# Float32r value products and batched modulation columns in the even layer of a two-layer hybrid attention kernel

## The chip, the cores and the metric

The kernel runs on one core of a Trainium2 chip. The metric is device time in microseconds. TensorE (PE, with its weight loads shown as PEld), VectorE (DVE), ScalarE (ACT), GpSimd (POOL) and the DMA queues (issued here mostly by SyncE, SP) each work through their own instructions in order and wait for one another by semaphores.

## The reference, cut to what matters

The program is one inference step of two layers over 128 prompt and 512 sample tokens with 1024 features. The part at stake is the attention of the even layer, 16 heads of 64 values: 8 latent heads (MLA, each with its own values) and 8 grouped heads (GQA, four heads share a value head). Sample queries read 128 cached and 512 own keys; prompt queries read only the 128 prompt keys.

```
def block(qi):
    s = jnp.einsum('bqhgd,bthd->bhgqt', qi, k).astype(jnp.float32) * scale
    p = jax.nn.softmax(s, axis=-1).astype(v.dtype)
    return jnp.einsum('bhgqt,bthd->bqhgd', p, v)
...
o_a = attend(q_a, k_a, v_a).reshape(B, S, MLA_W) * jax.nn.silu(g_a)
o_b = attend(q_bg, kb_all, vb_all).reshape(B, S, GQA_W) * jax.nn.silu(g_b)
return jnp.concatenate([o_a, o_b], axis=-1) @ w_out, new
```

The odd layer's input is a normalised x times a gain plus a shift; both come from the condition vectors by a product with 2048 columns of a modulation weight ("modulation columns").

## The kernel before, in words

All results are kept to float32 accuracy. Where a product runs in float32r, an operand is split into an upper part (rounded to float32r) and a lower part (the rest), and the products of the parts are added up in PSUM.

`even_attention` goes through 16 heads (h = 0 to 15; MLA first). A head has four sample query tiles of 128 queries and five key tiles of 128 keys. For each query tile, `head_scores` makes scores `s` [128 queries, 640 keys] (float32r products, L596) in one of two PSUM tiles; `softexp` takes the row maximum on VectorE (L603) and the exponential with its row sum on ScalarE (L606), the reciprocal of the sum on VectorE (L609); GpSimd multiplies the probabilities `p` by it (L616). For each key tile k, `head_T` transposes four blocks of `p` on TensorE (L623) into a PSUM tile `t1` (two of them), and one engine copies that into `pT` [128 keys, 512 queries] (ScalarE, L628; VectorE for k = 2, L626). `head_PV` multiplies with the 64 value columns (L634): two float32 products of 256 queries each, one into partitions 0 to 63 of PSUM tile `o`, one into 64 to 127, so that they lie side by side in the array. In the trace each float32 product is two PE instructions, so a key tile has four. At a head's end, VectorE multiplies the two halves of `o` into the gates `og` (L710).

`attention` writes the order out by hand: the transposition of key tile k+1 stands ahead of the value product of key tile k, and scores run about one head ahead (`more_scores`); a scheduler that simulates the program then fixes each engine's final order. Prompt heads are done four at a time by `prompt_quad` in four stages, spread over the first heads (two stages ahead of head 0, then two in each head), so that all four quads lie in the MLA half. `prep` (queries and keys of head h+2: a copy L760, transpositions, a split L315 or L754) and `side(h)` ride along. For h < 8, `side` calls `ada_cols` for the odd layer's modulation columns: 8 products and two transpositions on TensorE, then on VectorE a reduction (L186) and three operations on [128, 2] columns (L190, L193, L195). For h >= 8 it makes partial rows of the even gate (`ada_gate_part`), splits half of `og` for the output projection (`op_split`, ScalarE and VectorE L842) and, in heads 12 to 15, loads the four weight tiles of the projection's first 512 columns (`op_load` through `wload`: DMA, upper part on ScalarE L76, lower part on GpSimd L77).

Behind the attention, `mid` runs the output projection: `out_proj` first multiplies the first half of `og` (heads 0 to 7) of all five token tiles with weight tiles 0 and 1 (60 products, L83 to L85), then the second half with tiles 2 and 3.

Of the kernel before, what the change touches and what calls it, by code (L numbers as in the profile page):

```python
# [10 lines left out]
F32 = mybir.dt.float32  # L11
F32R = mybir.dt.float32r
# [25 lines left out]
class K:  # L38
# [3 lines left out]
    # ---------------------------------------------------------------- helpers  # L42
# [8 lines left out]
    def sumsq(self, src, n, w):  # L51
        """sum of squares over groups of w: src [128, n*w] in SBUF -> [128, n]"""
# [14 lines left out]
    def wload(self, src, n, w, pool=None, pre="w", bufs=2, cp=None):  # L67
        """stream a [128, n, w] weight tile and split it into two float32r parts"""
# [18 lines left out]
    def lin_tok(self, pieces, ncols, hh, hl, toks, evac, pool, tag="acc", bufs=5):  # L87
        """out[token, col] for token tiles toks; pieces: [(dram ap, nk)]"""
# [12 lines left out]
    def drain(self, toks, evac, lag=3):  # L101
        """evacuate psum; what evac returns is done lag tiles later"""
# [9 lines left out]
    def lin_feat(self, src, hh, hl, pool, tag="acc", bufs=5):  # L112
        """out[col (128), token (640)] in two psum tiles of 320 tokens"""
# [9 lines left out]
    def silu_from(self, out, src, shape, pool, other=None):  # L123
        """out = silu(src) (times other); src may be PSUM"""
# [8 lines left out]
    def rope(self, out, x, cos, sin, nh, w, pool, rep=1, dup=False):  # L133
        """out = rope(x), [128, nh, w] views; cos, sin [128, w / rep]"""
# [26 lines left out]
    # ---------------------------------------------------------------- adaLN  # L161
# [8 lines left out]
    def ada_cols(self, L, kk, pool, tag, bufs, raws=None, split=False):  # L170
        """shift and gain of feature tile kk as [128, 2] columns (sample, prompt)"""
# [10 lines left out]
        def rest():  # L182
            for i in range(2):
                nc.tensor.transpose(ps[:, 256 + 128 * i:384 + 128 * i], part[:, i * 128:i * 128 + 128], self.ident)
            red = self.st.tile([128, 2, 2], F32, tag="adar", name="adar", bufs=2)
            nc.vector.tensor_reduce(out=red, in_=ps[:, 256:512].rearrange("p (i g j) -> p i j g", i=2, g=4)[:, :, 0:2],  # L186
                                    axis=AX.X, op=ALU.add)
            vg, vs, vc = (V_EG, V_EBS, V_EBC) if L == "e" else (V_OG, V_OBS, V_OBC)
# [11 lines left out]

    def ada_gate_part(self, L, kk, pool, tag, bufs):
        """partial rows of the gate of feature tile kk"""
# [11 lines left out]
    def ada_gate_row(self, L, pool, tag, bufs):  # L214
        """sum of the partial rows of the gate, to DRAM"""
# [12 lines left out]
    def ada_gate_bc(self, L, to):  # L228
        """gate broadcast over partitions: [128, 2, 1024], sample and prompt"""
        self.gate = to  # L230
        for c in range(2):
            self.nc.sync.dma_start(to[:, c], self.gd[L][c:c + 1].to_broadcast([128, 1024]))

    # ---------------------------------------------------------------- body
    def run(self):
        tc, nc, A = self.tc, self.nc, self.A
        with ExitStack() as es:
# [12 lines left out]
            self.GS = {L: (main.tile([128, 8, 2], F32, name="G" + L), main.tile([128, 8, 2], F32, name="S" + L))  # L250
                       for L in "eo"}
# [27 lines left out]
    # ---------------------------------------------------------------- even layer  # L279
# [1357 lines left out]
```

## Time and profile before

| | us |
|---|---|
| runs: median, lowest, highest of 3 | 910.01, 910.0, 910.73 |
| profiled execution: span from its first to its last instruction | 905.8 |
| median of the runs less that span (what lies around it) | 4.2 |
| busy in the span: PE, DVE, ACT, POOL | 852.9, 541.2, 422.6, 396.6 |
| attention of the even layer, from 229 to 403 us of the span | 174 |

No time of the profiled execution beside its span is given, so the span is set against the runs. An engine's busy time is the time in which one of its instructions is shown as running; a PE instruction's shown length includes the way through the array, so PE is nearly always shown as busy, and what PE costs has to be read from the distance between starts.

### The profile page before, as it was taken

How to read it: one execution, taken by the hardware profiler on the slowest of the kernel's cores; microseconds unless marked ns; L12 is line 12 of the kernel's file. 1: busy time of each engine (PE TensorE's matmuls, PEld its weight loads, DVE VectorE, ACT ScalarE, POOL GpSimd, SP SyncE). 2: the span in 40 equal slices, each digit the busy share in tenths (PEclk: the TensorE clock that was granted, in tenths of full speed). 3: DMA queues.
4: the chain of work that ended last, by engine and by line, in shares of the span. 5: the costliest groups of instructions: out<-in, count | busy, mean ns of one | idle time of the engine just before them, and what ended most of it. 6: DMA issues, size and time to landing. Idle time of an engine off the chain costs nothing.

```text
span 905.8 us, 14374 instructions
## 1 busy us (share of the span) xinstructions
PE 852.9 (94%) x5418; PEld 707.2 (78%) x5418; DVE 541.2 (60%) x1125; ACT 422.6 (47%) x928; POOL 396.6 (44%) x302
## 2 busy tenths in 40 slices
PE   6999899979999999999999999999999899999997
PEld 2778788879776766668887889889989688778786
DVE  3773831993866877641386735077774736666765
ACT  5354523311655677752263324266554656443422
POOL 0144424751754646725535333422221946354930
PEclk9999999999999999999999999999999999999999
DMA  9821222220221222324412212222123122142503
GB/s 347 330 65 35 88 87 71 70 71 24 94 94 53 84 98 93 119 77 176 152 47 105 86 71 94 81 70 71 47 93 129 58 88 63 55 164 75 163 1 117
DMA packets 29641, 88.52 MB, mean 98 GB/s; under 512 B 3752, under 2 KB 6880, under 8 KB 29572
## 3 DMA queue, kind: packets, MB, share of 16 engines
q1 hardware_dynamic: 25904, 83.64, 26.4%
q10 hardware_dynamic: 3668, 3.96, 1.3%
q8 instruction: 43, 0.70, 0.3%
q14 instruction: 26, 0.21, 0.1%
HBM read 80.90 MB, written 6.68 MB: 97 GB/s over the span
## 4 chain that ended last, share of the span: by engine, by line
PE 74%; DVE 16%; issue 3%; ACT 3%; POOL 2%; DMA 1%; SPq 0%; POOLq 0%; ACTq 0%; DVEq 0%
PE acc L84 11%; PE acc L85 11%; PE acc L83 11%; PE s L596 7%; PE acc L1060 6%; PE o L634 5%; PE t L623 5%; PE acc L120 3%; PE o L1146 2%; PE pv L1460 2%; PE ada L177 1%; POOL wlo L77 1%; DVE nm L603 1%; PE gps L210 1%; PE acc L544 1%
## 5 line engine op out<-in xcount | busy, mean ns | idle before, releaser
L77 POOL TENSOR_TENSOR wlo<-raw,whi 128x1024 fp32r<-128x1024 f32 (+4 forms) x79 | 185.8, 2357 | 229.8 <-ACT whi L76 222.7
L85 PE MATMUL acc<-whi,Hl 128*128 128x512 f32 (+2 forms) x400 | 148.5, 373 | 1.6 <-DVE Hl L958 1.6
L84 PE MATMUL acc<-wlo,Hh 128*128 128x512 f32 (+2 forms) x400 | 149.2, 373 | 0.2 <-POOL wlo L77 0.2
L83 PE MATMUL acc<-whi,Hh 128*128 128x512 f32 (+2 forms) x400 | 138.9, 374 | 1.0 <-ACT qk L1064 1.0
L76 ACT CAST whi<-raw 128x1024 fp32r<-128x1024 f32 (+4 forms) x71 | 71.6, 1010 | 131.2 <-PE acc L85 80.5
L603 DVE TENSOR_REDUCE nm<-s 128x1 f32<-128x640 f32 (+1 forms) x104 | 80.9, 780 | 57.1 <-PE s L596 56.0
L616 POOL TENSOR_TENSOR p<-p,rs 128x640 f32<-128x640 f32 x64 | 79.7, 1256 | 64.2 <-DVE rs L609 62.6
L606 ACT ACTIVATE p<-s,nm 128x640 f32<-128x640 f32 (+1 forms) x104 | 79.4, 764 | 59.8 <-DVE nm L603 53.9
L85 PEld LDWEIGHTS acc<-whi,Hl 128*128 128x128 f32 x400 | 75.3, 188 | 14.7 <-DVE Hl L958 1.8
L83 PEld LDWEIGHTS acc<-whi,Hh 128*128 128x128 f32 x400 | 75.1, 188 | 14.0 <-ACT qk L1064 1.2
L84 PEld LDWEIGHTS acc<-wlo,Hh 128*128 128x128 f32 x400 | 75.4, 188 | 12.9 <-POOL wlo L77 0.6
L48 POOL TENSOR_TENSOR rs_r<-rs_h,mhalf 128x1 f32<-128x1 f32 (+4 forms) x39 | 35.6, 921 | 53.4 <-DVE rs_h L47 45.0
L623 PEld LDWEIGHTS t<-cst,p 128*128 128x128 f32 x320 | 34.6, 140 | 23.6 <-issue 22.1
L623 PE MATMUL t<-cst,p 128*128 128x128 f32 x320 | 51.3, 283 | 0.2 <-POOL p L616 0.2
L84 PE MATMUL acc<-wlo,oh 128*128 128x512 f32 (+1 forms) x124 | 48.1, 388 | 0.1
L85 PE MATMUL acc<-whi,ol 128*128 128x512 f32 (+1 forms) x124 | 47.8, 386 | 0.0
L83 PE MATMUL acc<-whi,oh 128*128 128x512 f32 (+1 forms) x124 | 46.7, 389 | 0.0
L628 ACT COPY pT<-t 128x512 f32<-128x512 f32 x64 | 37.1, 584 | 17.4 <-PE t L623 17.0
L120 PE MATMUL acc<-Hh,whi 128*128 128x320 f32 x128 | 31.3, 316 | 6.9 <-DVE og L129 6.9
L63 DVE TENSOR_REDUCE ssq<-sq 128x2 f32<-128x128 f32 (+3 forms) x19 | 11.5, 604 | 40.6 <-ACT sq L61 40.4
L885 ACT ACTIVATE junk<-xt 128x512 bf16<-128x512 f32 (+1 forms) x21 | 12.8, 610 | 49.0 <-DVE xt L883 37.7
L1060 PE MATMUL acc<-Hh,whi 128*128 128x320 f32 x128 | 32.5, 323 | 0.5 <-ACT v L1037 0.5
(380 smaller groups left out, 1983.2 us busy)
## 6 DMA issues: line engine op xcount, KB each, us to landing
adaw<-in_eada_ss_dram SPq DMA_DIRECT2D x16, 512.0 KB, 10.3
raw<-in_oada_ss_dram SPq DMA_DIRECT2D x16, 512.0 KB, 4.3
raw<-in_e_wG_dram SPq DMA_DIRECT2D x8, 512.0 KB, 3.3
raw<-in_eada_g_dram SPq DMA_DIRECT2D x8, 512.0 KB
raw<-in_e_wO_dram SPq DMA_DIRECT2D x8, 512.0 KB, 4.2
raw<-in_oada_g_dram SPq DMA_DIRECT2D x8, 512.0 KB, 3.5
raw<-in_o_wO_dram SPq DMA_DIRECT2D x8, 512.0 KB, 3.9
xT<-in_xT_dram SPq DMA_DIRECT2D x8, 320.0 KB, 5.8
```

The costliest lines, as they stand in the source:

```text
L76: (cp or nc.scalar.copy)(hi[:, 0:m], raw[:, 0:m])
L77: nc.gpsimd.tensor_tensor(out=lo[:, 0:m], in0=raw[:, 0:m], in1=hi[:, 0:m], op=ALU.subtract)
L83: mm(out, lhsT=lh, rhs=rh, start=first, stop=False)
L84: mm(out, lhsT=lh, rhs=rl, start=False, stop=False)
L85: self.mark = mm(out, lhsT=ll, rhs=rh, start=False, stop=last)
L120: mm(acc[j][:, 0:320], lhsT=a[:, k], rhs=b[:, k, j * 320:j * 320 + 320], start=f, stop=l)
L596: self.mark = self.nc.tensor.matmul(out[:, j, 0:w], lhsT=q[0:rows, qcols], rhs=k[0:rows, a:a + w], start=i == 0, stop=i == len(passes) - 1)
L603: nc.vector.tensor_reduce(out=nm, in_=s, axis=AX.XY, op=ALU.max, negate=True)
L606: nc.scalar.activation(out=p[:, 0:n].rearrange("p (a b) -> p a b", a=s.shape[1]), in_=s, func=AF.Exp, bias=nm, accum_out=sm)
L616: self.nc.gpsimd.tensor_tensor(out=p, in0=p, in1=rs.to_broadcast([128, 640]), op=ALU.mult)
L623: self.nc.tensor.transpose(tp[:, i * 128:i * 128 + 128], p[i][:, k * 128:k * 128 + 128], self.ident)
L1060: nc.tensor.matmul(acc[j][:, 0:320], lhsT=a[:, k], rhs=b[:, k, j * 320:j * 320 + 320], start=f, stop=l)
```

## The change

- Value products: each head's value columns are split into upper and lower parts that lie side by side, 128 columns (`values(h)`, one head ahead; for a GQA head only every fourth; the prompt's values `Pa`, `Pb` at the start). `head_T` ends in `split_T`: ScalarE writes the upper part of the transposed probabilities and VectorE the lower part. `head_PV` makes two float32r products of 512 queries, one with each part. Rows 0 to 63 of `o` then hold the upper-value sums and rows 64 to 127 the lower-value sums; at the head's end ScalarE copies the lower half, VectorE adds, GpSimd multiplies into the gates. `prompt_quad` is changed in the same way.
- Normalisation: the reciprocal is taken for two query tiles at once.
- The odd layer's shift and gain: `ada_cols` keeps only the reduction; `ada_close` finishes all eight feature tiles with three operations.
- `op_split` of the first half writes its lower part on GpSimd instead of VectorE.
- The projection's weight tiles 2 and 3 are loaded behind the attention (in `mid`, in a pool `R1b`), not in heads 14 and 15.
- Comments and docstrings are taken out, with no effect on the program.

```diff
         def rest():
...
-            red = self.st.tile([128, 2, 2], F32, tag="adar", name="adar", bufs=2)
+            red = self.gs[L][:, :, kk] if L == "o" else self.st.tile([128, 2, 2], F32, tag="adar", name="adar", bufs=2)
...
+            if L == "o":
+                return
...
+    def ada_close(self):
+
+        G, S = self.GS["o"]
+        col = lambda a: self.cols[:, a:a + 8, None].to_broadcast([128, 8, 2])
+        tt = self.nc.vector.tensor_tensor
+        tt(out=S, in0=S, in1=col(V_OBS), op=ALU.add)
+        tt(out=G, in0=G, in1=col(V_OBC), op=ALU.add)
+        self.nc.vector.scalar_tensor_tensor(out=G, in0=G, scalar=1.0, in1=col(V_OG), op0=ALU.add, op1=ALU.mult)
...
     def head_scores(self, T, ps, passes, i):
...
-        p, rs = self.softexp(T, s, 640, 10)
-        self.nc.gpsimd.tensor_tensor(out=p, in0=p, in1=rs.to_broadcast([128, 640]), op=ALU.mult)
+        if i % 2 == 0:
+            self.pair = [], T.tile([128, 2], F32, tag="sm", name="sm2", bufs=4)
+        tiles, sm = self.pair
+        p = self.softexp(T, s, 640, 10, sm[:, i % 2:i % 2 + 1])
+        tiles.append(p)
+        if i % 2:
+            nc.vector.reciprocal(sm, sm)
+            for j, x in enumerate(tiles):
+                nc.gpsimd.tensor_tensor(out=x, in0=x, in1=sm[:, j:j + 1].to_broadcast([128, 640]), op=ALU.mult)
...
-        pT = T.tile([128, 512], F32, tag="pT", name="pT", bufs=3)
-        if k == 2:
-            self.nc.vector.tensor_copy(pT, tp)
-        else:
-            self.nc.scalar.copy(pT, tp)
-        return pT
...
+        return self.split_T(T, tp)
+
+    def split_T(self, T, tp):
+        parts = [T.tile([128, 512], F32R, tag=n, name=n, bufs=2) for n in ("pTh", "pTl")]
+        self.split_psum(*parts, tp)
+        return parts
...
-            self.nc.tensor.matmul(o[64 * j:64 * j + 64, 0:256], lhsT=V[:, k, col:col + 64],
-                                  rhs=pT[:, 256 * j:256 * j + 256], start=k == 0, stop=k == 4,
-                                  tile_position=(0, 64 * j))
+            self.nc.tensor.matmul(o, lhsT=V(k), rhs=pT[j], start=k == 0 and j == 0, stop=k == 4 and j == 1)
...
                 if k == 2:
                     side(h)
+                    if h + 1 < nh:
+                        self.values(h + 1)
...
-            for j in range(2):
-                g = self.og[r, h // 2, 128 + 256 * j:384 + 256 * j]
-                nc.vector.tensor_tensor(out=g, in0=o[64 * j:64 * j + 64, 0:256], in1=g, op=ALU.mult)
+            s = T.tile([128, 512], F32, tag="os", name="os", bufs=1)
+            nc.scalar.copy(s[r], o[64:128])
+            nc.vector.tensor_tensor(out=s[r], in0=o[0:64], in1=s[r], op=ALU.add)
+            g = self.og[r, h // 2, 128:640]
+            nc.gpsimd.tensor_tensor(out=g, in0=s[r], in1=g, op=ALU.mult)
...
+        def split(out, src):
+            self.nc.vector.tensor_copy(out[..., 0, :], src)
+            self.nc.gpsimd.tensor_tensor(out=out[..., 1, :], in0=src, in1=out[..., 0, :], op=ALU.subtract)
...
+        def values(h):
+
+            if h < 8 or h % 4 == 0:
+                Sa[h] = T.tile([128, 5, 2, 64], F32R, tag="Sa", name="Sa", bufs=2)
+                split(Sa[h], Va[:, 0:5, 64 * h:64 * h + 64] if h < 8 else Vb[:, 0:5, 16 * (h - 8):16 * (h - 8) + 64])
+            else:
+                Sa[h] = Sa[h - 1]
+
+        self.values = values
+        values(0)
+        split(Pa, heads(Va[:, 5]))
+        split(Pb, heads(Vb[:, 5]))
...
-            if h >= 12:
+            if h in (12, 13):
                 self.op_load("e_wO", 0, h - 12)
...
-        self.nc.vector.tensor_tensor(out=lo, in0=src, in1=hi, op=ALU.subtract)
+        (self.nc.vector if m else self.nc.gpsimd).tensor_tensor(out=lo, in0=src, in1=hi, op=ALU.subtract)
...
+        self.Rb = self.tc.alloc_tile_pool(name="R1b", bufs=1, side="right", reuse_waits="tile")
+        for i in (2, 3):
+            self.op_load("e_wO", 0, i)
```

## Rows read from the trace of the kernel before

**Rows 1.** Windows: stretch, length, busy time (count) per engine, granted clock, DMA share, GB/s.

```profile
216.00:229.00 13.00, 11.72 (x77) 10.94 (x76) 6.02 (x14) 4.08 (x10) 1.39 (x2) 1.00 0.00 0
229.00:240.00 11.00, 9.55 (x86) 7.15 (x84) 9.59 (x19) 7.24 (x22) 10.06 (x9) 1.00 0.28 97
229.00:334.00 105.00, 102.26 (x818) 73.07 (x816) 77.23 (x168) 65.92 (x166) 61.90 (x50) 1.00 0.23 82
334.00:403.00 69.00, 67.28 (x542) 42.28 (x541) 43.32 (x85) 47.69 (x101) 40.31 (x29) 1.00 0.32 109
229.00:403.00 174.00, 169.54 (x1358) 115.35 (x1357) 120.55 (x252) 113.61 (x266) 102.22 (x79) 1.00 0.26 93
403.00:417.00 14.00, 14.00 (x64) 11.52 (x63) 3.17 (x6) 3.91 (x6) 1.22 (x1) 1.00 0.48 188
```

**Rows 2.** Chain that ended last, 250 to 285 us: start, length, what.

```profile
253.56 0.87 PE t L623 x8
...
268.42 1.01 PE o L634 x8
...
271.56 0.89 PE s L596 x6
...
280.97 0.58 PE o L634 x4
281.55 0.59 PE t L623 x4
```

**Rows 3.** Timeline of PE, 269 to 272 us: start, length, instruction.

```profile
269.86 0.60 PE L623 MATMUL t<-cst,p 128*128 128x128 f32 x4
270.21 0.83 PE L596 MATMUL s<-Ka,qh 96*128 96x320 f32 x4
270.88 0.46 PE L596 MATMUL s<-Ka,ql 96*128 96x320 f32 x2
271.18 0.38 PE L184 MATMUL ada<-cst,adap 128*128 128x128 f32 x2
```

**Rows 4.** VectorE groups by line and shape, 229 to 403 us: busy, mean ns | idle before.

```profile
L710 DVE TENSOR_TENSOR og<-o,og 64x256 f32<-64x256 f32 x32 | 13.4, 418 | 8.8 <-PE o L634 8.4
L626 DVE COPY pT<-t 128x512 f32<-128x512 f32 x16 | 10.9, 684 | 0.7 <-PE t L623 0.4
L609 DVE RECIPROCAL rs<-sm 128x1 f32<-128x1 f32 x62 | 9.7, 156 | 12.3 <-ACT p L606 11.7
L842 DVE TENSOR_TENSOR ol<-og,oh 128x512 fp32r<-128x512 f32 x5 | 6.3, 1292 | 0.0
...
L193 DVE TENSOR_SCALAR adat<-adar,cols 128x2 f32<-128x2 f32 x8 | 4.9, 614 | 0.0
L315 DVE TENSOR_TENSOR ql<-qtp,qh 128x512 fp32r<-128x512 f32 x6 | 4.1, 680 | 0.7 <-ACT qh L314 0.7
L190 DVE TENSOR_SCALAR So<-adar,cols 128x2 f32<-128x2 f32 x8 | 3.5, 441 | 0.2
L195 DVE TENSOR_SCALAR Go<-adat,cols 128x2 f32<-128x2 f32 x8 | 3.3, 412 | 0.1
L760 DVE CAST Ka<-kn 64x640 fp32r<-64x640 f32 x6 | 3.1, 519 | 0.1
L662 DVE COPY pTp<-t1p 128x512 f32<-128x512 f32 x4 | 2.7, 684 | 0.6 <-PE t1p L660 0.6
...
L782 DVE CAST kp<-kn 64x256 fp32r<-64x256 f32 x2 | 2.5, 1254 | 0.0
```

**Rows 5.** ScalarE groups of the same stretch.

```profile
L314 ACT CAST qh<-qtp 128x512 fp32r<-128x512 f32 x6 | 3.5, 585 | 2.3 <-PE qtp L764 2.2
```

**Rows 6.** GpSimd groups of the same stretch.

```profile
L616 POOL TENSOR_TENSOR p<-p,rs 128x640 f32<-128x640 f32 x63 | 78.5, 1256 | 49.5 <-DVE rs L609 47.8 <-PE t L623 1.0 <-PE o L634 0.4
L77 POOL TENSOR_TENSOR wlo<-raw,whi 128x1024 fp32r<-128x1024 f32 x4 | 9.5, 2364 | 3.7 <-ACT whi L76 3.7
```

**Rows 7.** DMA issues: count, KB each, median us to landing.

```profile
raw<-in_e_wO_dram SPq DMA_DIRECT2D x8, 512.0 KB, 4.2
```

More of the change, by code (lines that the diff above doesn't have):

```diff
@@ L249, in run @@
             self.sc = main.tile([128, 8, 32], F32, name="sc")
-            self.GS = {L: (main.tile([128, 8, 2], F32, name="G" + L), main.tile([128, 8, 2], F32, name="S" + L))
-                       for L in "eo"}
+            self.gs = {L: main.tile([128, 2, 8, 2], F32, name="gs" + L) for L in "eo"}
+            self.GS = {L: (t[:, 1], t[:, 0]) for L, t in self.gs.items()}
             self.gp = main.tile([128, 1024], F32, name="gp")
@@ L660, in prompt_quad, with attention @@
             nc.tensor.transpose(tp[:, j * 128:j * 128 + 128], p[:, j], self.ident)
-        pT = T.tile([128, 512], F32, tag="pT", name="pTp", bufs=3)
-        nc.vector.tensor_copy(pT, tp)
+        pT = self.split_T(T, tp)
         yield
         o = ps.tile([128, 512], F32, tag="t1", name="op", bufs=2)
-        for i in range(2):
+        for h in range(4):
+            c = slice(128 * h, 128 * h + 128)
             for j in range(2):
-                h = 2 * i + j
-                nc.tensor.matmul(o[64 * j:64 * j + 64, 128 * i:128 * i + 128], lhsT=V[:, 5, cols[h]:cols[h] + 64],
-                                 rhs=pT[:, 128 * h:128 * h + 128], start=True, stop=True, tile_position=(0, 64 * j))
+                nc.tensor.matmul(o[:, c], lhsT=V[h](5), rhs=pT[j][:, c], start=j == 0, stop=j == 1)
+        s = T.tile([128, 2, 128], F32, tag="os", name="ops", bufs=1)
+        v = lambda x, j: x.rearrange("p (a b c) -> p a b c", a=2, b=2)[:, :, j]
+        for j in range(2):
+            r = s[64 * j:64 * j + 64]
+            nc.scalar.copy(r, v(o[64:128], j))
+            nc.vector.tensor_tensor(out=r, in0=v(o[0:64], j), in1=r, op=ALU.add)
         g = self.og[:, m:m + 2, 0:128]
-        nc.vector.tensor_tensor(out=g, in0=o[:, 0:256].rearrange("p (a b) -> p a b", a=2), in1=g, op=ALU.mult)
+        nc.gpsimd.tensor_tensor(out=g, in0=s, in1=g, op=ALU.mult)
         yield
-    def attention(self, T, ps, P, prep, V, cols, side, quads):
+    def attention(self, T, ps, P, prep, V, side, quads):
         nc = self.nc
-        nh = len(cols)
+        nh = len(V)
         tiles = {}
@@ L830, in side @@
                 self.op_split(self.R, 0, h - 9)
-        self.attention(T, ps, P, prep, [Va] * 8 + [Vb] * 8, [64 * h for h in range(8)] + [64 * (h // 4) for h in range(8)],
-                       side, quads)
+        self.attention(T, ps, P, prep, V, side, quads)
     def op_split(self, P, m, t):
```

32 lines of the change are left out of this document (23 added, 9 removed).

## The prediction

> **What bounds the kernel now.** I read the windows first. The change lives in one stage, the even layer's attention, from 229 to 403 us; I split it at 334 us, where the MLA heads end and the GQA heads begin. TensorE is shown busy for 169.5 of 174 us and VectorE for 120.6, ScalarE for 113.6, GpSimd for 102.2 [rows 1]. So TensorE sets the pace, and the three others have 53 to 72 us to spare. The reader should see a second thing in the same rows: VectorE's room is uneven. In the MLA half it is busy for 77.2 of 105 us, in the GQA half for 43.3 of 69.
>
> Since a shown-busy TensorE says nothing of its cost, I then read the chain of waits, where a step's length is its distance to the next. Eight transpositions in a row cost 0.87 us, so four cost 0.435; eight value instructions in a row (two key tiles) cost 1.01, so one key tile costs 0.505 with one change of kind in it. But where four of the one and four of the other alternate, the pieces are 0.58 and 0.59, together 1.17 [rows 2]. So a key tile's value product costs 1.17 less 0.435, or 0.735 us, when it stands alone between transpositions. Most of the 80 key tiles stand so; pairs, as at 268.42, are rare in the chain.
>
> **TensorE's part.** After the change a key tile has two float32r products of 512 columns. Their price stands in the output projection: 64 in 14.0 us, 0.219 each [rows 1], so 0.44 a key tile. What the change of kind costs is read from scores, which are float32r among transpositions: from 269.86 to 271.18 four transpositions and six products take 1.32 us [rows 3], and the parts alone make 0.435 + 0.89 [rows 2]. Nothing is lost there beyond the parts. A key tile so saves 0.735 - 0.44 = 0.295 at most. The lower bound takes the price in pairs, 0.505 - 0.44 = 0.065. I take 0.22, nearer the upper end because nearly all stand alone, with a little kept back since the start of the next transpositions may still be late. 80 x 0.22 = 17.6 us (5 to 24). The prompt's products are few (four quads) and I cost them at nothing either way: eight products of 128 columns for eight instructions of half the width.
>
> The Trainium skill, "TensorE: Matmul & The Clock Gate", section "Part 3: Packing small matmuls — row/col tiling", speaks against this step: products in distinct column groups run concurrently, so the two 64-column products already share the array and widening them gives nothing back. By that rule the TensorE saving would be zero; the paired 0.505 against 0.44 lies close to it, the lone 0.735 does not.
>
> **VectorE, sums of durations** [rows 4]. Removed in the whole stage: the two multiplications into the gates 13.4 us; the copies for k = 2, 10.9; half of the reciprocals 4.9; the lower parts of the projection's operand 6.3; the three small operations 4.9 + 3.5 + 3.3 = 11.7, less three batched ones at about 0.6 = 1.8; the quads' copies 2.7. Together 48.1. Added: 80 lower parts of the transposed probabilities, the same kind of operation as L315, at 0.680 = 54.4; four more for the quads 2.7; 16 additions at a head's end, likewise 0.68 = 10.9; eight of half that width in the quads at 0.42 (L710) = 3.4, against four multiplications there of the same size, 1.7. Value casts: ten of 320 columns and two at the start. The trace has casts from SBUF at 0.519 for 640 columns and at 1.254 for 256; the slow ones fall where GpSimd is nearly always busy, so from 0.3 to 1.25 each; I take 0.75, 9 us (4 to 15). Added together 78.7, net +30.6, or 120.6 to 151 us, while TensorE would need 174 - 17.6 = 156.4.
>
> By halves, which decides: MLA loses 6.7 + 5.5 + 2.4 + 9.9 + 2.7 = 27.2 and gains 27.2 + 2.7 + 5.4 + 1.7 + 8 = 45.0, so 95.0 us, against a TensorE need of 105 - 8.8 = 96.2. GQA loses 6.7 + 5.5 + 2.4 + 6.3 = 20.9 and gains 27.2 + 5.4 + 1 = 33.6, so 56.0 against 69 - 8.8 = 60.2.
>
> On the casts the Trainium skill, "SBUF — State Buffer", section "Who interferes with whom", states that a VectorE copy or cast in a two-port mode and a GpSimd instruction exclude one another for a whole instruction. The 1.254 of L782, about one L616, agrees; that rule would put all twelve casts near the upper end, 15 us.
>
> **ScalarE and GpSimd.** ScalarE gains the 16 copies for k = 2 and the 16 at a head's end at 0.585 [rows 5], 18.7, up to 7 in the quads, and loses two weight casts: 113.6 to about 137. GpSimd [rows 6] gains 16 multiplications at 1.0 (512 of the 640 columns of 1.256), five lower parts at 1.2 (half of 2.364), about 9 of value parts and 2 of quads, and loses 2 x 2.4: 102.2 to about 130. Both stay below TensorE, but all four now stand at 83 to 97% of 156, and each head's work goes round all of them.
>
> **What else moves.** The start: `values(0)`, `Pa` and `Pb` come ahead of the first scores, 2 us on VectorE and 2.5 on GpSimd. From 216 to 229 these are busy for 6.0 and 1.4 of 13 us, from 229 to 240 for 9.6 and 10.1 of 11 [rows 1]. I cost it at nothing, hidden in the first stretch under the gates' products; in the second it would cost 2.5. Pairing the reciprocals delays a probability tile by one score, and scores run a head ahead: nothing. Weight tiles 2 and 3, now behind the attention, are wanted after 60 products, 60 x 0.219 = 13.1 us. On SP's queue their two transfers go ahead of the gate, residual and later weight loads; 4.2 [rows 7] + 1.2 (twice the 0.585 of half the size) + 2 x 2.4 = 10.2 us in series, with GpSimd free for 12.8 of 14 [rows 1]. Hidden by 3 us; without the cover, the same products would wait up to 5 us, and each load behind would come later.
>
> **The sum.** In the MLA half VectorE would have to be busy for 95.0 of 96.2 us. It works in order, and every lower part waits for ScalarE, so I let it reach 92 to 93%, against 74% now: 95.0 / 0.925 = 102.7, 2.3 us gained. In GQA at the same share 56.0 gives 60.5, TensorE's 60.2 is level with it; two engines that are level lose to each other, and I keep half the saving, 4.4. Together 6.7: span 905.8 to 899, and with the 4.2 us around the span 903.3. I say **903**, 897 to 908 for this case.
>
> **Rivals.**
>
> *TensorE's saving comes through whole.* For it: the scores' lead of a head covers much jitter, and VectorE's added work is regular, one lower part a key tile. Against it: 95.0 of 96.2. It gives 910 - 17.6 = **892** (888 to 897).
>
> *The way through the transposition tiles becomes the bound, and it is slower.* There are two PSUM tiles `t1`. One is now free only after transposition 0.435, upper part 0.585 and lower part 0.68, together 1.7 us with no queue, where before 1.02 did. Two tiles give a key tile each half of that plus the waits. GQA now does a key tile in 69 / 40 = 1.73 us, so this decides once the waits come to 1.75 us a tile, two operations ahead of it on VectorE or ScalarE; TensorE, in order, then stands. At 2.1 us it is 1.9 a key tile, 76 us for the half, and with no gain in MLA **917** (912 to 924). For it: VectorE's row maxima and the held casts stand in the same queue. Against it: the order can be spread over a head's scores.
>
> *Nothing is gained on TensorE, or what is gained is given back at the start and at the projection.* 17.6 less 17, or the pair's 0.065 x 80 = 5 less those 5: **910** (908 to 912).
>
> **How the numbers follow.** Likeliest 0.40, whole saving 0.20, slower loop 0.28, level 0.12. What can be told from no change is 0.2%, 1.8 us: faster is 0.40 + 0.20 = 0.60, same 0.12, slower 0.28. The range leaves out the far ends of the second and third case, 0.1 each: 891 to 917, which also holds the bounds of the value product and of the casts.
>
> **What would show it.** The stage should last 164 to 170 us, VectorE busy in it for over 145, the alternation of value products and transpositions below 1.0 us in the chain, and VectorE's lower parts named as what TensorE waits for, in the MLA half above all. Lone value products still near 0.7 would prove the first step wrong; VectorE below 140 us, the second; a TensorE stop after the first 60 products of the projection, the hidden load. The forecast fails if the scheduler's order leaves value products directly behind their lower parts.

## The result and the profile after

The changed kernel takes 932.73 us (median of 4 runs, 931.78 to 934.25) against 910.01 before (median of three runs; a fourth, slow one took 1385.36 us and is left out): ratio 1.0254 [1.0228, 1.0280], slower. The profiled execution has a span of 932.5 us against 905.8. The forecast was 903, with a range to 917.

To see where 26.7 us went, I marked five instructions in both traces: the first value product, the first one of head 8 (where MLA heads end and GQA heads begin), the last one, and the first and last product of the mLSTM's numerators.

| stretch, us | before | after | difference |
|---|---|---|---|
| start of span to first value product | 240.0 | 249.2 | +9.2 |
| MLA heads' value products | 96.3 | 108.7 | +12.4 |
| GQA heads' value products | 65.5 | 66.4 | +0.9 |
| last value product to mLSTM | 319.0 | 319.2 | +0.2 |
| mLSTM (code not changed) | 101.8 | 105.8 | +3.9 |
| rest | 83.2 | 83.2 | 0.0 |

The windows of the changed kernel for these stretches, for the forecast's 229 us to the projection, and for the projection's first 14 us (length, then busy time and count of PE, PEld, DVE, ACT, POOL, then granted clock, DMA share, GB/s):

```profile
222.00:249.17 27.17, 19.95 (x123) 16.95 (x122) 19.56 (x30) 11.60 (x32) 15.55 (x15) 0.75 0.13 41
249.17:357.85 108.68, 98.17 (x726) 80.62 (x725) 84.83 (x158) 77.06 (x182) 76.54 (x64) 0.97 0.28 92
357.85:424.25 66.40, 58.73 (x379) 43.14 (x379) 48.63 (x81) 46.67 (x98) 44.48 (x37) 1.00 0.19 58
249.17:424.25 175.08, 156.91 (x1105) 123.76 (x1103) 133.46 (x238) 123.73 (x280) 121.02 (x100) 0.98 0.24 79
...
425.00:439.00 14.00, 14.00 (x63) 11.54 (x63) 6.72 (x6) 6.76 (x10) 7.36 (x4) 1.00 0.31 100
229.00:425.00 196.00, 174.29 (x1206) 138.56 (x1207) 147.26 (x257) 134.02 (x311) 133.09 (x110) 0.95 0.23 77
```

The reader should see an absence: no engine is full. Where TensorE was busy for 169.5 of 174 us [rows 1], it now stands for 18 of 175, and VectorE, which was to become the bound, is busy for 84.83 of 108.68 us (78%) and 48.63 of 66.40 (73%). The chain of waits shows TensorE's own step in order, at 250 us:

```profile
250.45 0.23 PE o L657
250.68 0.44 PE t L646 x4
251.11 0.23 PE o L657
```

Two products of 0.23 and four transpositions of 0.44 make 0.90 us a key tile, where the alternation cost 1.17 [rows 2]. But in the GQA half value products, transpositions and scores make up only 41% of the chain (in the kernel before 77%), and for long pieces it leaves TensorE:

```profile
385.04 0.68 DVE pTl L326
385.72 0.73 DVE nm L615
386.45 0.60 DVE pTl L326
387.05 0.62 DVE os L737
387.67 0.26 DVE nm L615
387.94 0.40 issue
388.33 0.15 DVE sm L637
388.48 0.59 DVE pTl L326
...
389.72 0.69 DVE pTl L326
390.41 0.04 issue
390.45 0.51 PE o L657
390.96 0.44 PE t L646 x4
```

For over 5 us the chain runs through VectorE's queue, lower part, row maximum, lower part, head's end, and only then do a product and the next transpositions follow. The waits of the stretch from first to last value product say who stands (engine, what waits, for what; us, times, longest). The two longest, of GpSimd for VectorE's reciprocals and of these for ScalarE's row sums, are left out:

```profile
...
DVE pTl L326 <- ACT pTh L325: 13.2, 22, 2.5
PEld o L657 <- DVE pTl L326: 13.2, 27, 1.3
ACT pTh L325 <- PE t L646: 12.1, 20, 1.9
...
PE o L657 <- DVE pTl L326: 4.7, 10, 1.0
```

It is a ring: TensorE's products and their weight loads wait for VectorE's lower part, that for ScalarE's upper part, that for TensorE's transpositions. Each engine is idle in turn.

### The profile page after: what moved, and what is told of

Same layout as the page of the kernel before. It is cut to its first block, busy times and chain, and to the rows that moved or that the text cites. A ratio compares the mean times of both kernels' runs of the same rounds, so it can differ in the third digit from the quotient of the medians.

```text
span 932.5 us, 14134 instructions
## 1 busy us (share of the span) xinstructions
PE 860.7 (92%) x5258; PEld 732.2 (79%) x5258; DVE 568.8 (61%) x1131; ACT 443.9 (48%) x972; POOL 436.8 (47%) x339
## 4 chain that ended last, share of the span: by engine, by line
PE 66%; DVE 20%; ACT 6%; issue 5%; POOL 2%; DMA 1%; SPq 0%; ACTq 0%; POOLq 0%; DVEq 0%
PE acc L84 11%; PE acc L85 11%; PE acc L83 11%; PE acc L1119 6%; PE s L607 6%; PE acc L120 3%; PE o L657 3%; DVE nm L615 2%; PE t L646 2%; DVE pTl L326 2%; PE pv L1519 2%; PE o L1205 2%; ACT p L619 1%; PE ada L177 1%; POOL wlo L77 1%
## 5 line engine op out<-in xcount | busy, mean ns | idle before, releaser
L639 POOL TENSOR_TENSOR p<-p,sm 128x640 f32<-128x640 f32 x64 | 78.9, 1253 | 29.2 <-DVE sm L637 28.6
L326 DVE TENSOR_TENSOR pTl<-t,pTh 128x512 fp32r<-128x512 f32 x80 | 54.1, 684 | 10.1 <-ACT pTh L325 9.5
L325 ACT CAST pTh<-t 128x512 fp32r<-128x512 f32 x80 | 45.9, 587 | 18.0 <-PE t L646 12.1
L646 PE MATMUL t<-cst,p 128*128 128x128 f32 x320 | 48.8, 278 | 3.5 <-DVE ops L694 2.1
L646 PEld LDWEIGHTS t<-cst,p 128*128 128x128 f32 x320 | 39.3, 143 | 11.0 <-DVE pTl L326 1.4
L657 PE MATMUL o<-pTl,Sa 128*128 128x512 f32 x80 | 35.7, 446 | 5.2 <-DVE pTl L326 4.9
L657 PE MATMUL o<-pTh,Sa 128*128 128x512 f32 x80 | 36.3, 454 | 3.0 <-ACT pTh L325 1.4
L120 PE MATMUL acc<-Hh,whi 128*128 128x320 f32 x128 | 31.3, 316 | 6.9 <-DVE og L129 6.9
```

Source lines behind the costliest of these rows:

```text
L120: mm(acc[j][:, 0:320], lhsT=a[:, k], rhs=b[:, k, j * 320:j * 320 + 320], start=f, stop=l)
L326: self.nc.vector.tensor_tensor(out=lo, in0=src, in1=hi, op=ALU.subtract)
L639: nc.gpsimd.tensor_tensor(out=x, in0=x, in1=sm[:, j:j + 1].to_broadcast([128, 640]), op=ALU.mult)
L646: self.nc.tensor.transpose(tp[:, i * 128:i * 128 + 128], p[i][:, k * 128:k * 128 + 128], self.ident)
L657: self.nc.tensor.matmul(o, lhsT=V(k), rhs=pT[j], start=k == 0 and j == 0, stop=k == 4 and j == 1)
```

## The experiments

Eighteen kernels, each profiled once, on three chips. "First" is the first value product, "stretch" from first to last, both in us of the profiled execution; ratios are to the kernel before on the same chip. Part of "first" is not the attention's: VectorE's last gate multiplication (`og<-th,acc`), which stands ahead of it, ends between 224.6 and 227.2 us.

| run | first | MLA | GQA | stretch | span | ratio [95%] |
|---|---|---|---|---|---|---|
| before | 240.0 | 96.3 | 65.5 | 161.8 | 905.8 | |
| changed | 249.2 | 108.7 | 66.4 | 175.1 | 932.5 | 1.0254 [1.0228, 1.0280] |
| a1_start | 250.8 | 106.9 | 66.4 | 173.4 | 928.5 | 1.0229 [1.0177, 1.0282] |
| a2_single | 245.3 | 109.8 | 67.6 | 177.4 | 932.4 | 1.0249 [1.0193, 1.0304] |
| a3_nolow | 248.9 | 96.1 | 59.4 | 155.4 | 910.0 | 1.0034 [1.0006, 1.0062] |
| b1_pairs | 242.2 | 94.7 | 64.7 | 159.4 | 911.1 | 0.9992 [0.9971, 1.0013] |
| c1_load | 248.8 | 113.4 | 71.8 | 185.2 | 943.4 | 1.0389 [1.0351, 1.0428] |
| c2_hold | 248.2 | 102.6 | 64.3 | 166.9 | 922.1 | 1.0171 [1.0124, 1.0218] |
| c3_lag | 250.5 | 111.4 | 65.9 | 177.3 | 937.2 | 1.0302 [1.0261, 1.0343] |
| c4_scal | 244.5 | 107.5 | 66.6 | 174.0 | 923.7 | 1.0171 [1.0115, 1.0228] |
| c5_busy | 247.9 | 100.3 | 61.3 | 161.6 | 915.0 | 1.0102 [1.0068, 1.0135] |
| c6_hold | 248.1 | 99.5 | 61.8 | 161.2 | 918.8 | 1.0123 [1.0083, 1.0163] |
| b2_relief | 240.1 | 96.1 | 63.0 | 159.1 | 906.4 | 1.0001 [0.9974, 1.0028] |
| b12 | 242.3 | 94.4 | 62.9 | 157.2 | 905.1 | 0.9979 [0.9958, 1.0000] |
| d1_late | 245.9 | 110.9 | 67.5 | 178.4 | 934.6 | 1.0209 [1.0175, 1.0243] |
| d2_ring | 249.7 | 110.9 | 64.2 | 175.1 | 930.5 | 1.0188 [1.0167, 1.0209] |
| d3_lag2 | 247.3 | 104.0 | 62.9 | 166.9 | 923.9 | 1.0110 [1.0067, 1.0153] |
| d4_one | 242.3 | 84.1 | 56.7 | 140.8 | 890.7 | 0.9772 [0.9746, 0.9798] |
| e1_full | 241.7 | 105.0 | 63.7 | 168.6 | 920.8 | 1.0107 [1.0067, 1.0148] |
| e2_nine | 248.3 | 118.6 | 65.8 | 184.4 | 938.7 | 1.0322 [1.0281, 1.0362] |

### First round: which part of the change

**a3_nolow**, without lower parts:

```diff
-        parts = [T.tile([128, 512], F32R, tag=n, name=n, bufs=2) for n in ("pTh", "pTl")]
-        self.split_psum(*parts, tp)
-        return parts
+        hi = T.tile([128, 512], F32R, tag="pTh", name="pTh", bufs=3)
+        self.nc.scalar.copy(hi, tp)
+        return [hi, hi]
```

> The changed kernel without the lower parts of the transposed probabilities: both float32r products of a key tile read the upper part, so TensorE's work is the same, and VectorE has 84 operations of 0.68 us less; the output lacks that part. If the value products' wait for the lower part (ScalarE, then VectorE, two transposition tiles) is what eats TensorE's saving, the stage falls by 20 to 30 us: 902 to 913, and by more if the clock then stays up. If the start, the casts or the head's end is the cause, 926 to 933.

The stretch fell from 175.1 to 155.4 us:

```profile
248.93:404.37 155.44, 145.49 (x1106) 121.14 (x1104) 87.73 (x156) 122.51 (x282) 121.72 (x101) 1.00 0.27 89
```

The lower part so costs 19.7 us, more than the stretch's whole loss of 13.3 (the third buffer for the upper part, which this kernel has too, did nothing by itself; see d2_ring). What is left is also instructive. TensorE's products are those of the changed kernel, and its busy time is 145.5 us, against 158.8 of 161.8 in the kernel before, whose window is:

```profile
239.99:401.77 161.78, 158.78 (x1274) 107.41 (x1270) 110.19 (x233) 105.89 (x243) 92.15 (x70) 1.00 0.26 93
```

So 13.3 us of TensorE's busy time are saved. But it now waits for 10 us where it waited for 3, so that 6.4 come through, nearly all in the GQA half (65.5 to 59.4; MLA 96.3 to 96.1). And the first value product is nearly as late as in the changed kernel: the 9 us of the start are another matter.

**a1_start and a2_single** took the start apart: the value casts ordered behind the first row maxima, and a reciprocal for each query tile.

```diff
-        values(0)
-        split(Pa, heads(Va[:, 5]))
...
+        with self.tc.issue_after(self.nm.ins):
+            self.first()
```

> The changed kernel with one thing moved: the first value casts (Sa of heads 0 and 1, Pa, Pb) stand on VectorE behind the row maxima of the first scores instead of ahead of them. If the late start (first value product at 249.2 us instead of 240.0) comes from these casts, 4 to 9 us come back: 924 to 929. If it comes from the paired reciprocals or from the cut clock alone, the time stays at 931 to 934.

```diff
-        if i % 2 == 0:
-            self.pair = [], T.tile([128, 2], F32, tag="sm", name="sm2", bufs=4)
...
+        p, rs = self.softexp(T, s, 640, 10)
+        nc.gpsimd.tensor_tensor(out=p, in0=p, in1=rs.to_broadcast([128, 640]), op=ALU.mult)
```

> The changed kernel with the reciprocals taken for each query tile again. If the pairing holds back the first transpositions (235.0 us instead of 229.5) and later ones, 3 to 8 us come back: 925 to 930. If VectorE's number of instructions is what counts, 32 more of 0.15 us make it up to 3 us slower: 932 to 936.

The casts' place changed nothing (first value product 250.8; 24.4 us behind the last gate, 24.5 in the changed kernel). Single reciprocals brought it from 249.2 to 245.3 (18.9 behind the last gate), but the loop took most of that back: last value product 422.7 against 424.3 us. The whole run is no shorter; from there to the mLSTM this kernel takes 323.4 us, the changed one 319.2, and why stays open. Five more runs have such a stretch of 323 to 324 us (c1_load, c3_lag, c6_hold, d1_late, d3_lag2), so stages are compared here by their own marks, not by whole runs.

**b1_pairs** asked the opposite question of the kernel before: its fp32 products in pairs of key tiles, with one more buffer for the transposed probabilities.

```diff
-                if k:
-                    self.head_PV(o, V[h], cols[h], pt.pop(k - 1), k - 1)
+                if k in (2, 4, 5):
+                    with self.tc.issue_after(self.lastT.ins):
+                        for x in ((0, 1), (2, 3), (4,))[(2, 4, 5).index(k)]:
+                            self.head_PV(o, V[h], cols[h], pt.pop(x), x)
```

> The kernel before, with the value products of two key tiles queued behind the same transposition where that can be, so that some 20 pairs (before: 5) stand side by side; the work is the same. If a lone value product in column groups loses 0.23 to 0.29 us to the changes of kind around it, some 15 more pairs give 3 to 4 us: 906 to 907. If the changes of kind cost nothing in the end, 910, or up to 915 as products wait for their pair.

The stretch is 2.4 us shorter, the whole run the same (0.9992), not the 3 to 4 us faster that were expected.

### Second round: what of the lower part costs

Three mechanisms can make it dear: VectorE's load, the transposition tile in PSUM that is now held until VectorE is through, and the products' wait. Operations whose result nobody reads separate them.

**c1_load, c2_hold**: a subtraction for each tile, unread, from the upper part in SBUF (c1_load), and from the transposition tile in PSUM (c2_hold, `in0=tp`). The edit of c1_load:

```diff
+        hi, lo = [T.tile([128, 512], F32R, tag=n, name=n, bufs=b) for n, b in (("pTh", 3), ("pTl", 1))]
+        self.nc.scalar.copy(hi, tp)
+        self.nc.vector.tensor_tensor(out=lo, in0=hi, in1=hi, op=ALU.subtract)
+        return [hi, hi]
```

> The changed kernel with both value products reading the upper part; VectorE still makes an operation of the lower part's kind for each key tile (84 in all), but from the upper part in SBUF, and nobody reads its result: VectorE's load is back, the PSUM tile is free after ScalarE, no product waits for VectorE. Left out is the lower part of the probabilities (the upper is counted twice). From first value product to the projection the changed kernel takes 175.1 us, without lower parts 155.5. Theory A (the products wait for the lower part, or the transposition tile is held by it): 156 to 160 here, whole run 911 to 917. Rival B (VectorE's 54 us of added work as such delays row maxima and all else in its queue): 170 or more, 926 to 934.

> As the run before, but the unread operation reads the transposition tile in PSUM, so that the tile is held until VectorE is done; still no product waits for the lower part. Theory A1 (two transposition tiles, each held by ScalarE and then VectorE): the stretch comes to 168 to 175 us, the run to 924 to 933. Theory A2 (the products wait for the lower part): 156 to 162, the run 911 to 918. If both count, in between; what is missing to the changed kernel's 175.1 is the products' wait.

c2 gave 166.9 us, so load and held tile together make 11.5, and what is left to 175.1, 8.2 us, is the products' wait. c1 gave 185.2, more than the changed kernel, at a granted clock of 0.94, and doesn't measure what it was to measure. VectorE's groups say why (busy, mean ns), first c1_load, then c5_busy, the run that replaced it:

```profile
L652 DVE TENSOR_TENSOR pTl<-pTh 128x512 fp32r<-128x512 f32 x84 | 93.3, 1111 | 6.5 <-ACT pTh L651 3.8
```

```profile
L653 DVE TENSOR_REDUCE mx<-pTh 128x1 f32<-128x512 f32 x84 | 55.9, 679 | 8.1 <-ACT pTh L651 7.1
```

With both sources in SBUF the subtraction took 1.11 us in the mean (0.66 at the least), where one from PSUM takes 0.68, and GpSimd's multiplications of probabilities grew from 1.25 to 1.42. The reduction took 0.66 to 0.69, and GpSimd stayed at 1.25. The Trainium skill, "SBUF — State Buffer", section "Who interferes with whom", says that a VectorE instruction with two SBUF inputs contends with a GpSimd instruction that reads SBUF, and that a reduction never does; both rows agree.

**c5_busy, c6_hold**: load alone by a reduction from SBUF, and holding alone by one column of the transposition tile.

```diff
+        self.nc.vector.tensor_reduce(out=mx, in_=hi.bitcast(F32), axis=AX.X, op=ALU.max)
```

```diff
+        self.nc.vector.tensor_tensor(out=mx, in0=tp[:, 0:1], in1=hi[:, 0:1], op=ALU.subtract)
```

> Both value products read the upper part, as before in this series (the lower part of the probabilities is left out, the upper counted twice). VectorE gets one row maximum over the 512 columns of the upper part in SBUF for each transposition tile, about as long as a lower part (0.6 to 0.8 us), which nobody reads; the PSUM tile is free after ScalarE. Without lower parts the stretch took 155.4 us, with an unread operation on the PSUM tile 166.9. Theory B (the load on VectorE's queue makes these 11.5 us): 163 to 169 here. Theory A1 (the tile is held through VectorE's queue): 155 to 159.

> As the run before, but VectorE's unread operation is one column of the transposition tile: the tile is held until VectorE's queue comes to it, at hardly any load (about 0.06 us each, 5 us in all). Theory A1 (held tiles): 162 to 168 us. Theory B (load): 155 to 159. If both runs of this pair fall between, load and hold work together: the tile is late because the queue is long.

```profile
247.85:409.48 161.63, 148.37 (x1105) 123.67 (x1104) 135.75 (x240) 123.42 (x282) 121.79 (x101) 0.98 0.26 86
```

```profile
248.12:409.33 161.21, 148.21 (x1106) 120.98 (x1105) 97.19 (x240) 122.88 (x282) 121.48 (x101) 1.00 0.26 86
```

Load alone (DVE 135.75 us) costs 6.2 us, holding alone (DVE 97.19, of which the one-column operations are 12, not the 5 expected) 5.8. Neither forecast of a single cause held; the two add, 12.0 against c2's 11.5. The waits show each way. With load alone ScalarE's exponentials wait 12.5 us for row maxima, 7.1 without lower parts; with holding alone the transpositions' weight loads wait 4.5 us and the transpositions themselves 3.2 for the unread column. The clock is in these sizes: 1.00 in the stretch without lower parts and with holding, 0.98 with load, 0.99 with both, 0.98 in the changed kernel. The ratios of whole runs rise in the same order, 1.0034, 1.0102, 1.0123, 1.0171, 1.0254, though they hold what lies outside the stretch too.

**c3_lag, d2_ring, d3_lag2, e2_nine** looked for a remedy of that wait: a key tile more between lower part and products.

```diff
-        parts = [T.tile([128, 512], F32R, tag=n, name=n, bufs=2) for n in ("pTh", "pTl")]
+        parts = [T.tile([128, 512], F32R, tag=n, name=n, bufs=b) for n, b in (("pTh", 3), ("pTl", 2))]
...
-                if k:
-                    self.head_PV(o, V[h], pt.pop(k - 1), k - 1)
+                with self.tc.issue_after(self.lastT.ins):
+                    for x in ((), (), (0,), (1,), (2,), (3, 4))[k]:
+                        self.head_PV(o, V[h], pt.pop(x), x)
```

> The changed kernel with each key tile's value products held back behind the transpositions of the key tile after the next, three buffers for the upper part and nine instead of ten probability tiles: the products have a key tile more of time before they want the lower part, while transposition tiles are held as before. Theory A2 (products wait): the stretch falls from 175.1 to 160 to 166 us, the run to 916 to 924. Theory A1 (tiles held) or B (VectorE's load): 172 to 178, the run 929 to 936.

With nine probability tiles (for room) this gained nothing, 177.3. Casting the prompt's values a quad at a time (d1_late, below) frees the room for ten. d2_ring is the buffers alone, d3_lag2 buffers and lag.

> As the run before, with three instead of two buffers for the upper part of the probabilities. Held tiles and load gave 166.9 us with an upper part in three buffers, the changed kernel with two takes 175.1. Theory C (ScalarE, which writes the upper part, waits for a buffer that the products still read): 167 to 170. Theory A2 (the products wait for the lower part itself): 173 to 177, no change.

> As the run before, and each key tile's products held back behind the transpositions of the key tile after the next, at ten probability tiles. The first run with this lag had nine and took 177.3 us. Theory A2 (wait for the lower part, which a lag hides): 165 to 170. Rival (a fixed order of the products makes TensorE wait for other things, so that nothing is gained): 174 to 178.

```profile
247.27:414.17 166.90, 150.50 (x1097) 118.54 (x1095) 136.01 (x241) 123.52 (x280) 122.27 (x103) 0.99 0.24 80
```

The third buffer alone: the last value product comes at 424.8 us, in d1_late without it at 424.3, so nothing (the stretch is 3.3 us shorter than d1_late's only because its first product is 3.7 later). With the lag the stretch falls from 175.1 to 166.9, as much as c2 has. The wait itself shows it, in d2_ring and then in d3_lag2:

```profile
PEld o L657 <- DVE pTl L326: 13.3, 27, 1.0
```

```profile
PEld o L657 <- DVE pTl L326: 4.6, 9, 1.0
```

So the products waited for the lower part itself. What had hidden this in c3 was the missing tenth probability tile:

> The kernel whose products are held back by a key tile and which took 166.9 us, with nine instead of ten probability tiles. The first kernel with that lag (nine tiles, prompt values cast at the start) took 177.3. If the tenth tile, that is the scores' lead, makes the difference: 174 to 178 us, the run 930 to 937. If it was the prompt's value casts: 166 to 169, the run 923 to 928.

```profile
248.25:432.62 184.37, 160.12 (x1097) 125.67 (x1095) 141.26 (x241) 123.60 (x280) 122.03 (x103) 0.94 0.22 73
```

One tile less, and 166.9 became 184.4, beyond what was expected (178). Some of it may be the clock, 0.94 in this stretch against 0.99. Nine tiles are slow with the prompt's casts at the start as well (c3_lag, 177.3, at a clock of 0.96); what the tile costs apart from the clock isn't separated.

### Third round: the start, and what would be faster

**c4_scal** has single reciprocals and the value casts on ScalarE; **d1_late** the prompt's casts one quad at a time; **e1_full** both, with the lag.

```diff
-            self.nc.vector.tensor_copy(out[..., 0, :], src)
+            self.nc.scalar.copy(out[..., 0, :], src)
```

> The changed kernel with a reciprocal for each query tile and the value casts on ScalarE instead of VectorE (so that none is held off by a GpSimd instruction). The first value product came at 249.2 us in the changed kernel, at 245.3 with single reciprocals, at 240.0 before the change. Theory (VectorE's held casts delay the first scores): 240 to 243. Rival (the wait is for TensorE's clock or GpSimd): 244 to 247. For the whole run the loop decides: 928 to 934, since 4 us won at the start were not kept to the end when the reciprocals alone were undone; if they are kept now, 922 to 927.

```diff
-        split(Pa, heads(Va[:, 5]))
-        split(Pb, heads(Vb[:, 5]))
...
+                t = T.tile([128, 4, 2, 64], F32R, tag="Pq", name="Pq", bufs=1)
+                split(t[:, 0:n], heads(Va[:, 5])[:, 4 * m:4 * m + 4] if m < 2 else heads(Vb[:, 5])[:, m - 2:m - 1])
```

> The changed kernel with the prompt's value parts cast for one quad at a time, in that quad's third stage, instead of all at the start: of the casts only the first head's stay ahead of the loop. First value product 249.2 us in the changed kernel, 240.0 before the change. Theory (the casts of the prompt's values delay the start): 244 to 246. Rival (paired reciprocals and the clock's fall, the casts hardly): 248 to 250. The loop itself should stay at 174 to 177 us in either case, the run at 926 to 934.

> Both parts kept: products held back by a key tile with three buffers for the upper part, prompt values cast per quad, and besides single reciprocals and value casts on ScalarE. With the first two alone the stretch took 166.9 us, from a first value product at 247.3. If the start's 4 us now stay won: first product at 242 to 244, stretch 165 to 169, projection from 408 to 412, ratio 1.003 to 1.009. Rival (they are given back in the loop, as with single reciprocals alone): projection from 413 to 417, ratio 1.009 to 1.014. For a faster run than before the change the held tiles' and the load's 12 us would have to go too, which neither expects.

The first value product comes at 244.5, 245.9 and 241.7. Moving the casts to ScalarE adds little to single reciprocals (245.3) at the start, as the rival had it; but the loop then keeps the gain, the last value product comes at 418.5 and the run takes 925.1 us. Late casts take back 3.2 us, single reciprocals 3.9. Counted from the last gate, the four kernels with late casts and paired reciprocals (d1_late, d2_ring, d3_lag2, e2_nine) are 2.0 to 4.0 us earlier than the changed kernel, the one with single reciprocals alone 5.6. But the kernels without lower parts, whose casts stand at the start, are 2.5 earlier too, so the late casts' gain isn't clear of what else changes. All of these had 6.8 to 10.2 us at half clock between the last gate and the first value product, the changed kernel 13.7. In e1_full, with both and the casts on ScalarE, the start is within 1.7 us of the kernel before, and here the clock stayed at 1.00, as it did there; what the edits and what the clock brought isn't told apart. Alone, the reciprocals are mostly and the late casts wholly lost again in the loop (last value product 422.7 and 424.3, against 424.3); in e1_full they are kept: the projection starts at 410.6, as the theory had it. The whole run is at 1.0107, above the theory's range: against the kernel before it lost 2.5 us in the odd layer ahead of the mLSTM and 3.9 in it.

**b2_relief, b12**: the kernel before with the batched columns and the lower parts on GpSimd, without and with pairs.

```diff
-        self.nc.vector.tensor_tensor(out=lo, in0=src, in1=hi, op=ALU.subtract)
+        (self.nc.vector if m else self.nc.gpsimd).tensor_tensor(out=lo, in0=src, in1=hi, op=ALU.subtract)
```

> The kernel before with two other parts of the change: the odd layer's modulation columns finished in one batch, and the lower parts of the first half of the projection's operand on GpSimd; value products stay in fp32 and column groups. 16 us of VectorE work leave the stage. Theory (TensorE sets the pace of the kernel before, VectorE had room): no change, ratio 0.997 to 1.003. Rival (VectorE's queue delayed scores there too): stage 2 to 4 us shorter, ratio 0.995 to 0.998.

> The kernel before with the same two parts and, besides, its fp32 value products in pairs of key tiles (this alone shortened the stretch from 161.8 to 159.4 us at an unchanged whole). Theory (changes of kind on TensorE are what can be saved, other engines have room): stretch 158 to 160, ratio 0.996 to 1.000. If relief and pairs help each other: stretch below 158, ratio below 0.996.

Relief alone shortens the stretch by 2.7 us, as the rival said, but not the run, where the mLSTM, whose code is the same, is 2.8 longer. With pairs the stretch is 157.2 and the ratio 0.9979 [0.9958, 1.0000]: perhaps a little faster.

**d4_one**: one product for each key tile.

```diff
+        hi = T.tile([128, 512], F32R, tag="pTh", name="pTh", bufs=4)
+        self.nc.scalar.copy(hi, tp)
+        return [hi]
...
+        self.nc.tensor.matmul(o, lhsT=V(k), rhs=pT[0], start=k == 0, stop=k == 4)
```

> The changed kernel with one value product for each key tile, with the probabilities rounded to float32r (their lower part is left out; the values keep both parts), value casts on ScalarE and single reciprocals. 80 products of 0.23 us and all lower parts are gone. Without lower parts but with two products the stretch took 155.4 us. If TensorE bounds that one: 137 to 145, the run 892 to 902. If ScalarE, GpSimd and the way through the transposition tiles bound it: 148 to 154, the run 902 to 910.

```profile
242.32:383.17 140.85, 130.00 (x1018) 108.15 (x1014) 84.31 (x177) 125.49 (x291) 121.85 (x100) 0.98 0.30 99
```

140.8 us, in the range for a stretch bound by TensorE: with 80 products fewer it is 14.6 us shorter than without lower parts, and TensorE's busy time 15.5 us. So TensorE seems to set the pace once VectorE is out of the ring; the casts on ScalarE and the single reciprocals may have a share. 894.67 against 914.55 us on that chip, 0.9772: faster than both kernels, at the price of probabilities in one float32r part.

## Why the prediction was wrong, step by step

*TensorE's part: right.* 13.3 us of busy time saved where 17.6 (5 to 24) were forecast, and 0.90 a key tile in the chain. The zero that the prediction worked out from the Trainium skill, "TensorE: Matmul & The Clock Gate", section "Part 3: Packing small matmuls — row/col tiling" (products in distinct column groups run concurrently), did not come. That rule isn't refuted by it, since the change also went from float32 to float32r and the runs don't tell the two apart. b1_pairs kept float32 and got 2.4 us.

*The sums of busy time: right.* From 229 us to the projection VectorE is busy for 147.3 us (forecast 151), ScalarE 134.0 (137), GpSimd 133.1 (130). The twelve value casts took 6.8 us of VectorE, where 9 (4 to 15) were forecast; most were not held up.

*The weight tiles behind the attention: right.* TensorE is busy for 14.00 of the 14 us from 425.

*Start casts and paired reciprocals, both costed at nothing: wrong*, by 9.2 us together with the clock. The casts are not hidden under the gates' products. VectorE's timeline, changed kernel, then the kernel before:

```profile
223.78 0.88 DVE L129 TENSOR_TENSOR og<-th,acc 128x320 f32<-128x320 f32 x2
224.69 0.36 DVE L842 CAST Sa<-Va 128x320 fp32r<-128x320 f32 x1
224.96 0.41 DVE L842 CAST Pa<-Va 128x512 fp32r<-128x512 f32 x1
225.29 0.90 DVE L842 CAST Pb<-Vb 128x128 fp32r<-128x128 f32 x1
226.11 1.43 DVE L842 CAST Sa<-Va 128x320 fp32r<-128x320 f32 x1
227.46 1.53 DVE L615 TENSOR_REDUCE nm<-s 128x1 f32<-128x640 f32 x2
```

```profile
224.06 0.88 DVE L129 TENSOR_TENSOR og<-th,acc 128x320 f32<-128x320 f32 x2
224.85 0.81 DVE L603 TENSOR_REDUCE nm<-s 128x1 f32<-128x640 f32 x1
```

They begin behind the last gates and stand ahead of the first row maxima, with the second head's cast (1.43) among them. Their order isn't all of it: a1_start had the row maxima first and its first value product was no earlier. Pairing lets the pair's first probability tile wait for the second's sum, and at the start there is no lead of scores yet to cover that; this way is argued, not shown (the first transposition came at 235.2 us with single reciprocals, at 235.0 with pairs). Single reciprocals gave 3.9 us of it back, late casts 3.2. "Scores run a head ahead" was true of the loop only. The third part is the clock. The chain to the first value product has these pieces at half clock:

```profile
229.24 3.58 PE s L607 x12
...
242.08 1.97 PE s L607 x6
```

In the kernel before, at a clock of 1.00, twelve such products cost half:

```profile
242.40 1.75 PE s L596 x12
```

Six cost 0.89 there [rows 2]. These two pieces alone are 2.9 us longer.

*The sum: here the forecast failed.* "I let it reach 92 to 93%" took VectorE's share as what sets the loop, and a share as given. It reached 78 and 73%, and the loop lost 19.7 us to the lower part: about 6.2 because row maxima stand behind lower parts in VectorE's queue, 5.8 because a transposition tile comes free only when that queue has come to it, 8.2 because products stand behind their lower part in TensorE's order (measured one by one they make 20.2). The last is what the forecast named as its own condition of failure, without a price. Against a 6.4 us gain of the rest, that makes the stretch 13.3 us longer.

*The slower rival was right in kind and too small.* It had held tiles alone, put them in the GQA half and gave 917, at most 924; the run took 932.7. The GQA half lost 0.9 us (7.0 to the lower part, less the 6.1 saved); the MLA half, where it saw no change, lost 12.4. Besides the lower part, MLA has a stop at 333 us, where ScalarE's weight cast waits for its transfer with an upper part and an exponential behind it, and TensorE stands for 2.4 us:

```profile
329.52 4.21 DMA raw<-in_e_wO_dram
...
335.35 0.80 ACT p L619 x2
336.14 0.04 issue
336.19 1.34 PE s L607 x4
```

Moving that load was not tried, nor was a third transposition tile.

*The clock stood in no term.* It costs part of the start, part of MLA and, as far as the runs show, the mLSTM's 3.9; see below.

The sizes come from one profile each, and whole runs of one kernel spread by 8 us and more (909.1 to 917.2 without lower parts, 906.9 to 917.7 in 22 runs of the kernel before on one chip), so that 6.2 and 5.8 are equal as far as this can tell; c5_busy's profile, moreover, is of the fastest of its four runs. What each half-clock stretch costs in the attention is not separated from the waits that go with it.

## What to carry to other kernels

Work moved from the engine that sets the pace to one with room is not priced by busy time when it lands in a ring that the first engine waits on. Price the ring: what stands ahead in the new engine's queue, which buffer is now held longer, and how far behind the consumer follows. Operations that nobody reads separate the three for a run each, and if the consumer's wait is one of them, let it follow a step later, but not at the cost of the producers' lead: here the lag won 8 us and one probability tile fewer lost 17, some of it perhaps to the clock.

## What was not expected of the hardware

TensorE's granted clock fell to 0.50, the lower of its two levels, in the changed kernel in four stretches of 6.8 us where the kernel before kept 1.00: from 227.1, 240.7, 336.3 and 742.5 us; a shorter one of 3.4 us came at 824.4. Ahead of the first three TensorE was busy for 5.02, 4.88 and 4.14 of 6.8 us, at a clock of 1.00, with a stop of 2.4 us in the last. The windows of the changed kernel:

```profile
220.30:227.10 6.80, 5.02 (x34) 4.51 (x32) 3.86 (x8) 0.77 (x2) 1.98 (x2) 1.00 0.00 0
227.10:233.90 6.80, 4.66 (x19) 4.63 (x20) 4.54 (x8) 3.23 (x8) 3.18 (x5) 0.50 0.00 0
...
329.50:336.30 6.80, 4.14 (x25) 3.14 (x26) 3.83 (x6) 4.50 (x9) 5.45 (x5) 1.00 0.37 122
336.30:343.10 6.80, 6.80 (x28) 6.46 (x29) 3.60 (x7) 3.71 (x9) 4.89 (x5) 0.50 0.22 77
742.50:749.30 6.80, 5.82 (x17) 4.97 (x18) 2.94 (x7) 3.08 (x10) 5.62 (x8) 0.50 0.43 137
```

The one from 742.5 is in code that the change doesn't touch, and what goes before is the same in both kernels. The stretch ahead of it, changed kernel, then the kernel before, and there the stretch that answers to 742.5 too:

```profile
735.70:742.50 6.80, 4.88 (x25) 3.96 (x23) 6.04 (x9) 4.24 (x7) 6.80 (x8) 1.00 0.08 19
```

```profile
713.00:719.80 6.80, 4.88 (x25) 3.96 (x23) 6.04 (x9) 4.25 (x7) 6.80 (x8) 1.00 0.07 19
719.80:726.60 6.80, 5.83 (x30) 4.95 (x31) 4.66 (x9) 4.60 (x14) 6.36 (x11) 1.00 0.42 141
```

PE was busy for 4.88 of 6.80 us in both, yet the clock fell in one, with 17 matrix instructions in the next 6.8 us, and stayed in the other, with 30. The Trainium skill, "TensorE: Matmul & The Clock Gate", section "Part 1: The HAM clock gate (the "warmup" mystery)", has it that the gate's look at the engine runs free of the kernel's start; the two rows agree with that. What it costs can be read in the mLSTM, whose code is the same in all twenty kernels. It takes 101.5 to 101.9 us in the three whose clock stays at 1.00 there (before, a1_start, a3_nolow); 102.8 to 103.1 in the twelve with one half-clock stretch of 3.4 us, at its start or some 80 us later; 104.6 in the two with both (b2_relief, c2_hold); and 105.7 to 105.8, 3.9 more than in the kernel before, in the three with 6.8 us at the start and 3.4 later (changed kernel, b1_pairs, e1_full). Two kernels that differ by 4 us in all may so differ by nothing that was changed.
